# Layer 1's raw weight loads: a pool of four buffers in place of three, and each load issued one part sooner

## The chip, the cores and the metric

The kernel runs on one core of a Trainium2 chip. The metric is the device time of one execution, in microseconds (us); lower is better. Engines are named as in the profile: PE (TensorE), DVE (VectorE), ACT (ScalarE), POOL (GpSimd) and SP, the sequencer on which nearly all DMAs are issued, one after the other.

## What is computed

Two layers over 512 tokens of width 2048, in float32. Layer 0 is forgetting attention, layer 1 is RWKV-7 time mixing; each is a gated branch that is added to x. Layer 1 is the one that the change touches:

```python
def rwkv7_branch(h, v_first, mu, w_in, w0, w1, w2, ...):
    xx = shift(h) - h
    xr, xw, xk, xv, xa, xg = (h + xx * mu[i] for i in range(6))
    r, k, v, z = xr @ w_in[0], xk @ w_in[1], xv @ w_in[2], xg @ w_in[3]
    w = exp(-exp(-softplus(-(w0 + tanh(xw @ w1) @ w2)) - 0.5))
    v = v + (v_first - v) * sigmoid(v0 + (xv @ v1) @ v2)
    a = sigmoid(a0 + (xa @ a1) @ a2)
    kk = l2norm_per_head(k * k_k);  k = k * (1 + (a - 1) * k_a)
    # per head, over time: S = S*w + (S @ -kk) (kk*a)^T + v k^T;  y = S @ r
    ...
    return (group_norm(y) * lnx_w + lnx_b + bonus) * silu(z) @ w_out
```

## The kernel before

Activations lie transposed, a column block of 128 features by 512 tokens. Every big product is made at near float32 precision out of three matmuls in a rounded format: a weight w is split into `whi` (w rounded) and `wlo` (w - whi), an activation into `hi` and `lo`, and `mm3` issues hi*whi, hi*wlo and lo*whi.

**The backbone.** `backbone` walks over a list of weight tiles (2048 x 128). In layer 1 these are 10 tiles of wk1, then 16 each of wr, wv1, wz1 and wo1. A tile comes in four *parts* of 128 x 512 (256 KB), so layer 1 has 296 parts, counted here from 0; one part feeds 12 matmuls. For each part `fetch(n)` does three things in turn: a DMA on SP into a `raw` buffer, then on ACT `whi` = round(raw), then on DVE `wlo` = raw - whi. `raw` has three buffers, `whi` and `wlo` four each. `fetch(n)` is started when the matmuls of part n-4 begin; its ACT step stands 4.5 units of the kernel's own clock later, and not before part n-1 is split and part n-4 used up.

**The order.** The kernel is written out at build time by a small scheduler (`Flow`): tasks yield delays and take turns on a clock that counts PE work alone (`InOrder.clock`). PE, ACT and DVE then execute in the order in which the scheduler wrote them; SP's DMAs stand in one queue as well, in an order that follows it. An instruction that waits holds up all behind it on its engine.

**The side work.** Beside the backbone runs the chain that ends in the recurrence, in `side`: the low-rank products (`lora_k`, `lora_up`; beside wk1), `keys` for 16 blocks (beside wr), `invert` (triangular inverses of four groups, the last of them, group 3, on DVE: tiles `lane` and `lt`) and `inverse`, `stage` (beside wv1), and the chunked recurrence `recur` (beside wv1 and wz1). In `keys` a mean over a head is a pair of PE matmuls `S<-mhi,blkr` and `S<-mlo,blkr`, which wait for `mhi` from ACT and `mlo` from DVE. In `inverse` the matmuls `x<-qt,us` wait for `us` from ACT. In `recur` the tile `xs` is a DVE copy of x that the next PE matmuls (`x<-xs,QP`) read.

Almost all instructions are issued through one helper, so the profile gives them all one line (L90); tiles tell them apart.

Of the kernel before, what the change touches and what calls it, by code (L numbers as in the profile page):

```python
# [9 lines left out]
F = mybir.dt.float32  # L10
R = mybir.dt.float32r
# [6 lines left out]
P = 128  # L18
# [3 lines left out]
WK = 4  # L22
# [109 lines left out]
def body(ctx, tc, a, out, dbg=None, stop=0):  # L132
# [5 lines left out]
    cp = ctx.enter_context(tc.tile_pool(name="cp", bufs=1))  # L138
    wp = ctx.enter_context(tc.tile_pool(name="wp", bufs=4))
    cur = {}  # L140
    ast = ExitStack()
    ctx.callback(ast.close)

# [91 lines left out]
    def split(hi, lo, src):  # L235
        act_hi(hi, src)
        dve.tensor_tensor(out=lo, in0=src, in1=hi, op=OP.subtract)
# [3 lines left out]
        lo = cur["a"].tile([P, T], R, tag="lo", name="lo")  # L241
        return hi, lo

    def wload(src, nk, m, tag="", pool_=None, bufs=None):
        q = pool_ or wp
        raw = q.tile([P, nk, m], F, tag="raw" + tag, name="raw", bufs=bufs or (3 if q is wp else None))
        sp.dma_start(raw, src)
        hi = q.tile([P, nk, m], R, tag="whi" + tag, name="whi", bufs=bufs)
        lo = q.tile([P, nk, m], R, tag="wlo" + tag, name="wlo", bufs=bufs)
        split(hi, lo, raw)  # L250
        return hi, lo

    def mm3(o, w, k, x, first, last, m0=0, m1=P):
        wh, wl = w
        xh, xl = x
        pe.matmul(o, wh[:, k, m0:m1], xh, start=first, stop=False)
        pe.matmul(o, wl[:, k, m0:m1], xh, start=False, stop=False)
        pe.matmul(o, wh[:, k, m0:m1], xl, start=False, stop=last)

    def proj(src, A):  # L260
        o = bank("pj")
        for h in range(0, KT, WK):
            w = wload(src[:, h:h + WK, :], WK, P)
            for k in range(WK):
                mm3(o, w, k, A[h + k], h + k == 0, h + k == KT - 1)
        return o

    mdone = set()

# [49 lines left out]
    def backbone(fl, tiles, at, ready, ends, pairs=(), lead=6, pre=()):  # L319

        units, i = [], 0
        while i < len(tiles):
            us = [[(n, k) for k in range(t[4] if len(t) > 4 else 0, KT)]
                  for n, t in enumerate(tiles[i:i + 1 + (i in pairs)], i)]
            units += us[0][:PLEAD] if len(us) > 1 else us[0]
            for u, v in zip(us[0][PLEAD:], us[1] if len(us) > 1 else ()):
                units += [u, v]  # L330
            if len(us) > 1:
                units += us[1][KT - PLEAD:]
            i += len(us)
        starts = {}
        for i, k in units:
            starts.setdefault((i, k // WK), (i, k))
        parts = list(starts)
        ws, used = {}, set()

        def fetch(n):  # L340
            i, h = parts[n]
            raw = wp.tile([P, WK, P], F, tag="raw", name="raw", bufs=3)
            sp.dma_start(raw, tiles[i][0][:, h * WK:h * WK + WK, :])
            yield 4.5
            while n and parts[n - 1] not in ws or n > 3 and parts[n - 4] not in used:
                yield 0.2
            hi = wp.tile([P, WK, P], R, tag="whi", name="whi")
            lo = wp.tile([P, WK, P], R, tag="wlo", name="wlo")
            act_hi(hi, raw)
            yield 1  # L350
            dve.tensor_tensor(out=lo, in0=raw, in1=hi, op=OP.subtract)
            ws[parts[n]] = hi, lo

        def ending(task, i):
            yield from task
            freed.add(i)

        for n, w in enumerate(pre):
            ws[parts[n]] = w
        for n in range(len(pre), 4):  # L360
            for _ in fetch(n):
                pass
        for n in range(4, len(parts)):
            at.setdefault(starts[parts[n - 4]], []).append(fetch(n))
        last = {id(t[1]): i for i, t in enumerate(tiles)}
        banks, seen = {}, set()
        for i, k in units:
            src, acts, done, j = tiles[i][:4]
            first = i not in seen
            while first and i > 1 and i - 2 not in freed:  # L370
                fl.t += 0.2
                fl.run()
            if first:
                seen.add(i)
                banks[i] = bank("pj")
                at.setdefault((i, max(k, KT - lead)), []).append(ending(done(j, banks[i], i), i))
            for t in at.pop((i, k), ()):
                fl.start(fl.t, t)
            fl.run()
            while (id(acts), k) not in ready or (i, k // WK) not in ws:  # L380
                fl.t += 0.2
                fl.run()
            mm3(banks[i], ws[i, k // WK], k % WK, acts[k], first, k == KT - 1)
            if k % WK == WK - 1:
                used.add((i, k // WK))
            if last[id(acts)] == i:
                spent.add((id(acts), k))
            if k == KT - 1:
                ends.add(i)
# [3 lines left out]
    A = []  # L393
    act_pool("ap0", 16)
    psum("ps0", pj=2, ss=1, S=2, tr=2, pv=1)
    with ExitStack() as s0:
        lq = s0.enter_context(tc.tile_pool(name="lq", bufs=2, reuse_waits="tile"))
        cst, zst = ExitStack(), ExitStack()
# [5 lines left out]
        with tc.tile_pool(name="st0", bufs=2, reuse_waits="tile") as q:  # L404
# [67 lines left out]
            def z_load(n):  # L472
                if n < len(zt):
                    j, g = zt[n]
                    zraw[n] = wp.tile([P, WK, P], F, tag="raw", name="raw", bufs=3)
                    sp.dma_start(zraw[n], a["wz"][j][:, g * WK:g * WK + WK, :])

            def z_split(n):
# [571 lines left out]

    fl = Flow()
    NK = KT - len(ks)
    mq = ctx.enter_context(tc.tile_pool(name="mq", bufs=2, reuse_waits="tile"))
    vst = ExitStack()
    ctx.callback(vst.close)
# [533 lines left out]
    def recur(q):  # L1589
        for m in range(NG * NCH):  # L1590
            g, u, c = m // NCH, m // UC % NU, m % UC
            last = m % NCH == NCH - 1
            while m not in staged or not last and m + 1 not in svs:
                yield 0.1
            if "v" in dbg:
                print("chain", m, fl.t, len(ends))
            yield from hop()
            SV, L, qp, gp, dec, tok = staged.pop(m)
            nSV = None if last else svs[m + 1]
            if c == 0:  # L1600
                y = bank("y")
                y4 = y.rearrange("p (j c t) -> p j c t", j=NJ, c=UC)
            x = bank("x").rearrange("p (a j t) -> p a j t", a=2, j=NJ)
            for j in range(NJ):
                for h in range(2):
                    pe.matmul(x[HS[h], 0, j], L[h][:, j, 0, :], SV[h][:, j, :],
                              start=True, stop=True, skip_group_check=True)
            xs = q.tile([P, NJ, C], F, tag="xs", name="xs", bufs=2)
            dve.tensor_copy(xs, x[:, 0])
            for j in range(NJ):  # L1610
                for h in range(2):
                    pe.matmul(y4[HS[h], j, c], SV[h][:, j, :], L[h][:, j, 1, :],
                              start=j == 0, stop=False, skip_group_check=True)
            for h in range(2):
                s = HS[h]
                for j in range(0 if last else NJ):
                    pool.tensor_scalar(nSV[h][s, j, :], SV[h][s, j, :], dec[s, j, c:c + 1],
                                       1.0, op0=OP.mult, op1=OP.mult)
            yield from hop()
            for j in range(NJ):  # L1620
                for h in range(2):
                    pe.matmul(x[HS[h], 1, j], qp[h][:, j, :], xs[:, j, :],
                              start=True, stop=True, skip_group_check=True)
            for h in range(2):
                dve.tensor_copy(SV[h][HS[h]], x[HS[h], 1])
            yield from hop()
            if not last:
                x = bank("x").rearrange("p (a j t) -> p a j t", a=2, j=NJ)
                for j in range(NJ):
                    for h in range(2):  # L1630
                        pe.matmul(x[HS[h], 0, j], tok[:, j, h, :], SV[h][:, j, :],
                                  start=True, stop=True, skip_group_check=True)
                for h in range(2):
                    s = HS[h]
                    dve.tensor_tensor(out=nSV[h][s], in0=nSV[h][s], in1=x[s, 0], op=OP.add)
            for j in range(NJ):
                for h in range(2):
                    pe.matmul(y4[HS[h], j, c], SV[h][:, j, :], gp[h][:, j, :],
                              start=False, stop=True, skip_group_check=True)
            svs.pop(m)  # L1640
            free["chunk"] += 1
            if c == UC - 1:
                fl.start(fl.t + 0.5, normed(q, g, u, y))
# [216 lines left out]
```

## Time and profile before

| what | value |
|---|---|
| median of 3 runs | 2413.06 us (2410.73 to 2416.13) |
| profiled execution, its own time | 2413.1 us |
| profiled execution, span of the core | 2411.2 us |
| PE busy | 2308.0 us, 96% of the span |
| DVE, ACT, POOL busy | 1605.5, 1257.2, 686.2 us |
| mean bytes moved | 199 GB/s |

PE is the engine that is nearly always busy: what it does not do in the span is 103 us. Busy time of PE is counted from the first to the last of pipelined matmuls, and a matmul at half the clock is busy twice as long, so that the granted clock has to be read beside it.

### The profile page before, as it was taken

To read this page: it belongs to the slowest core of one execution; us is meant where nothing else is said; L and a number is where in the kernel's file an instruction comes from. 1 tells how busy PE (TensorE), PEld (TensorE's weight loads), DVE (VectorE), ACT (ScalarE), POOL (GpSimd) and SP (SyncE) were. 2 spreads that over 40 slices of the span, in tenths; PEclk is the share of its full clock that TensorE was granted. 3 is DMA by queue.
4 is the path that set the end of the run, shared out by engine and by line. 5 is a ranking of instruction groups with operands and counts; after the bars stand their busy time and mean duration, and the time that the engine had idled before them with its cause. 6 is when DMAs were issued, how large, how long until landed. Compare 5 with 4: busy or idle time off the path is not lost. (4 is left out here: it accounts for less than half of the span.)

```text
span 2411.2 us, 39377 instructions
## 1 busy us (share of the span) xinstructions
PE 2308.0 (96%) x13626; PEld 1807.8 (75%) x13626; DVE 1605.5 (67%) x2850; ACT 1257.2 (52%) x2300; POOL 686.2 (28%) x1114
## 2 busy tenths in 40 slices
PE   6999899999999999998999898899999999999999
PEld 4787677877778778886777676677777777777787
DVE  6886678888888745335797567667477776765322
ACT  4435655555565544225646777764345556665221
POOL 0002332533324210110042207771245535450000
PEclk8999999999999999999999999989999999999999
DMA  8864366666666456444755999886867766644543
GB/s 304 329 224 158 108 198 216 212 216 222 201 222 213 133 181 205 137 147 141 227 183 185 301 270 278 262 253 192 237 184 198 212 177 189 173 132 153 160 137 96
DMA packets 388151, 480.22 MB, mean 199 GB/s; under 512 B 146032, under 2 KB 217840, under 8 KB 384112
## 3 DMA queue, kind: packets, MB, share of 16 engines
q1 hardware_dynamic: 386288, 475.08, 63.4%
q0 software_dynamic: 1664, 2.63, 0.3%
q8 instruction: 108, 1.77, 0.3%
q14 instruction: 91, 0.75, 0.1%
HBM read 381.63 MB, written 95.95 MB: 198 GB/s over the span
## 5 line engine op out<-in xcount | busy, mean ns | idle before, releaser
L90 PE MATMUL pj<-hi,whi 128*128 128x512 f32 x2416 | 987.5, 409 | 14.2 <-ACT hi L90 8.2
L90 PE MATMUL pj<-hi,wlo 128*128 128x512 f32 x2416 | 960.2, 397 | 9.1 <-DVE wlo L90 9.1
L90 PE MATMUL pj<-lo,whi 128*128 128x512 f32 x2416 | 960.1, 397 | 0.0
L90 DVE TENSOR_TENSOR wlo<-raw,whi 128x512 fp32r<-128x512 f32 (+2 forms) x628 | 474.5, 763 | 261.4 <-ACT whi L90 258.0
L90 ACT ACTIVATE whi<-raw 128x512 fp32r<-128x512 f32 (+2 forms) x628 | 394.2, 634 | 405.2 <-PE pj L90 229.3
L90 PEld LDWEIGHTS pj<-hi,whi 128*128 128x128 f32 x2416 | 459.6, 190 | 120.4 <-ACT hi L90 9.0
L90 PEld LDWEIGHTS pj<-lo,whi 128*128 128x128 f32 x2416 | 458.4, 190 | 108.7 <-DVE lo L90 0.6
L90 PEld LDWEIGHTS pj<-hi,wlo 128*128 128x128 f32 x2416 | 460.1, 190 | 105.1 <-DVE wlo L90 12.4
L90 DVE CUSTOM_DVE_ANT_0 wm<-wm,cb 128x1024 f32<-128x1024 f32 x128 | 156.7, 1225 | 0.3
L90 POOL TENSOR_SCALAR SV<-SV,dec 64x64 f32<-64x64 f32 x224 | 93.4, 439 | 105.9 <-DVE SV L90 71.7
L90 ACT ACTIVATE pr<-Sm,mx 128x128 f32<-128x128 f32 (+3 forms) x128 | 71.5, 558 | 85.6 <-POOL mx L90 81.6
L90 POOL TENSOR_SCALAR mx<-mx 128x1 f32<-128x1 f32 x128 | 65.7, 513 | 154.9 <-DVE mx L90 118.0
L90 POOL TENSOR_SCALAR pr<-pr,rc 128x128 f32<-128x128 f32 (+3 forms) x128 | 87.6, 685 | 33.0 <-DVE rc L90 28.6
L90 POOL TENSOR_TENSOR lt<-lane 128x30 f32<-128x30 f32 (+14 forms) x90 | 62.7, 697 | 83.9 <-DMA lane<-mld 77.1
L90 DVE CUSTOM_DVE_ANT_0 Sm<-S,cmask 128x128 f32<-128x128 f32 (+3 forms) x128 | 62.0, 484 | 36.0 <-PE S L90 35.4
L90 POOL TENSOR_TENSOR bk<-bk,eI 128x512 f32<-128x512 f32 x32 | 36.1, 1128 | 112.3 <-PE S L90 75.3
L90 POOL TENSOR_TENSOR lane<-lane,lt 128x30 f32<-128x30 f32 (+14 forms) x90 | 65.7, 730 | 7.1
L90 PE MATMUL S<-k,q 128*128 128x128 f32 (+7 forms) x256 | 62.4, 326 | 0.0
L90 PE MATMUL tr<-ident,pr 128*128 128x128 f32 x320 | 57.2, 277 | 4.3 <-DVE pT L90 1.4
L90 POOL TENSOR_TENSOR acc<-acc,sq 128x512 f32<-128x512 f32 x14 | 18.1, 1295 | 150.8 <-ACT sq L90 150.8
L90 PEld LDWEIGHTS tr<-ident,pr 128*128 128x128 f32 x320 | 41.6, 142 | 25.4 <-ACT pT L90 6.9
L90 DVE SCALAR_TENSOR_TENSOR hp<-pj,gate,hp 128x512 f32<-128x512 f32 x16 | 12.0, 751 | 68.9 <-PE pj L90 68.9
(325 smaller groups left out, 3272.8 us busy)
## 6 DMA issues: line engine op xcount, KB each, us to landing
wm<-in_wmodT SPq DMA_DIRECT2D x132, 512.0 KB, 4.3
raw<-in_wz SPq DMA_DIRECT2D x128, 256.0 KB, 3.8
raw<-in_wo SPq DMA_DIRECT2D x128, 256.0 KB, 3.5
raw<-in_wv SPq DMA_DIRECT2D x124, 256.0 KB, 3.8
wm<-in_wmodT SPq DMA_DIRECT2D x30, 1024.0 KB, 6.9
raw<-in_wk SPq DMA_DIRECT2D x96, 256.0 KB, 3.7
raw<-in_wr SPq DMA_DIRECT2D x64, 256.0 KB, 5.1
raw<-in_wq SPq DMA_DIRECT2D x56, 256.0 KB, 3.6
```

Source lines behind the costliest of these rows:

```text
L90: self.last = f(*a, **k)
```

## The change

`raw` leaves the pool `wp` and gets a pool of its own, made anew for each layer: three buffers in layer 0, four in layer 1. `fetch(n)` is started at part n-1-`cur["rn"]`: part n-4 as before in layer 0, part n-5 in layer 1. To make room (a raw buffer takes 2 KB of each partition), `xs` of the recurrence has one buffer in place of two. Two helpers that nothing called (`wload`, `proj`) are gone.

```diff
+    def raw_pool(name, bufs):
+
+        rst.close()
+        cur["r"] = rst.enter_context(tc.tile_pool(name=name, bufs=bufs, reuse_waits="tile"))
+        cur["rn"] = bufs
...
         def fetch(n):
             i, h = parts[n]
-            raw = wp.tile([P, WK, P], F, tag="raw", name="raw", bufs=3)
+            raw = cur["r"].tile([P, WK, P], F, tag="raw", name="raw")
             sp.dma_start(raw, tiles[i][0][:, h * WK:h * WK + WK, :])
...
         for n in range(4, len(parts)):
-            at.setdefault(starts[parts[n - 4]], []).append(fetch(n))
+            at.setdefault(starts[parts[max(0, n - 1 - cur["rn"])]], []).append(fetch(n))
...
+    raw_pool("rw0", 3)
...
-                    zraw[n] = wp.tile([P, WK, P], F, tag="raw", name="raw", bufs=3)
+                    zraw[n] = cur["r"].tile([P, WK, P], F, tag="raw", name="raw")
...
     NK = KT - len(ks)
+    raw_pool("rw1", 4)
...
-            xs = q.tile([P, NJ, C], F, tag="xs", name="xs", bufs=2)
+            xs = q.tile([P, NJ, C], F, tag="xs", name="xs", bufs=1)
```

PE's order is the same in both kernels. What moves are the DMAs on SP and the splits on ACT and DVE. Three places follow.

SP, where the parts of wk1 end and those of wr begin (`ip`, `kt`, `aa` are the loads of the first block of `keys`). Before:

```order
694 L90 DMA hp<-mxd 128x512 x3
695 L90 DMA raw<-in_wk 128x512
696 L90 DMA ip<-ipd 128x4x128
697 L90 DMA kt<-kTd 128x512
698 L90 DMA aa<-aad 128x512
699 L90 DMA raw<-in_wr 128x512
700 L90 DMA hp<-mxd 128x512 x3
701 L90 DMA raw<-in_wr 128x512
```

With the change:

```order
692 L90 DMA hp<-mxd 128x512 x3
693 L90 DMA raw<-in_wr 128x512
694 L90 DMA ip<-ipd 128x4x128
695 L90 DMA kt<-kTd 128x512
696 L90 DMA aa<-aad 128x512
697 L90 DMA raw<-in_wr 128x512
698 L90 DMA hp<-mxd 128x512 x3
699 L90 DMA raw<-in_wr 128x512
```

The rows of loads stand in the same places, but each carries the next part: where the last part of wk1 stood there is now the first of wr. So it is in the whole of layer 1: nearly every other DMA has one raw load more ahead of it.

ACT, at the sixth block of `keys` (`sq`, `eI`, `aa`, `mhi`, `t` are its steps; `r<-pj` and `m<-hp` belong to other tasks). Before:

```order
1149 L90 ACTIVATE whi<-raw 128x512
1150 L90 ACTIVATE gab<-S 64x256 x4
1151 L90 ACTIVATE sq<-kt,vecs 128x512
1152 L90 ACTIVATE eI<-ip 128x8x64
1153 L90 ACTIVATE whi<-raw 128x512
1154 L90 ACTIVATE aa<-aa,oka,vecs 128x512
1155 L90 ACTIVATE r<-pj 128x512
1156 L90 ACTIVATE mhi<-sq 128x512
1157 L90 ACTIVATE m<-hp,omu 128x512
1158 L90 ACTIVATE whi<-raw 128x512
```

With the change:

```order
1146 L90 ACTIVATE whi<-raw 128x512
1147 L90 ACTIVATE gab<-S 64x256 x4
1148 L90 ACTIVATE whi<-raw 128x512
1149 L90 ACTIVATE sq<-kt,vecs 128x512
1150 L90 ACTIVATE eI<-ip 128x8x64
1151 L90 ACTIVATE aa<-aa,oka,vecs 128x512
1152 L90 ACTIVATE whi<-raw 128x512
1153 L90 ACTIVATE r<-pj 128x512
1154 L90 ACTIVATE mhi<-sq 128x512
```

The split that stood behind `eI` now stands ahead of `sq`, and the one that stood behind `m` now stands ahead of `r` and `mhi`. In 9 of the 16 blocks of `keys` one split more stands ahead of `mhi`.

DVE, where the inversion of group 3 begins (`lt`, `lane`; `lo<-hp` is a split of an activation). Before:

```order
1782 L90 STREAM_TRANSPOSE t_15902<-qt_13171 32x256
1783 L90 TENSOR_TENSOR wlo<-raw,whi 128x512
1784 L90 TENSOR_TENSOR lt<-lane 128x30
1785 L90 TENSOR_TENSOR lane<-lane,lt 128x30
1786 L90 TENSOR_TENSOR lo<-hp,hi 128x512
1787 L90 TENSOR_TENSOR wlo<-raw,whi 128x512
1788 L90 TENSOR_TENSOR lt<-lane 128x58
```

With the change:

```order
1788 L90 STREAM_TRANSPOSE t_15912<-qt_13181 32x256 x2
1789 L90 TENSOR_TENSOR wlo<-raw,whi 128x512 x2
1790 L90 TENSOR_TENSOR lt<-lane 128x30
1791 L90 TENSOR_TENSOR lane<-lane,lt 128x30
1792 L90 TENSOR_TENSOR lo<-hp,hi 128x512
1793 L90 TENSOR_TENSOR wlo<-raw,whi 128x512
1794 L90 TENSOR_TENSOR lt<-lane 128x58
```

Part 99's `wlo` stood behind the first `lt` (row 1787 before); now it stands ahead of it, together with part 98's, and the row behind carries part 100.

## Rows read from the trace of the kernel before

**Rows 1.** The page's head: span and busy time of each engine.

```profile
span 2411.2 us, 39377 instructions
PE 2308.0 (96%) x13626; PEld 1807.8 (75%) x13626; DVE 1605.5 (67%) x2850; ACT 1257.2 (52%) x2300; POOL 686.2 (28%) x1114
```

**Rows 2.** Stretches: length, busy (count) by engine, granted clock, DMA share, GB/s.

```profile
1140.00:1200.00 60.00, 60.00 (x260) 48.66 (x259) 44.60 (x61) 42.54 (x66) 3.66 (x10) 1.00 0.79 239
...
1366.00:1600.00 234.00, 210.87 (x1360) 162.31 (x1360) 161.16 (x206) 169.74 (x312) 134.87 (x185) 0.96 0.90 264
1600.00:1660.00 60.00, 53.19 (x451) 41.18 (x450) 43.37 (x91) 27.45 (x55) 24.07 (x33) 0.91 0.73 222
1660.00:1760.00 100.00, 95.28 (x855) 75.80 (x855) 48.32 (x91) 37.29 (x73) 16.92 (x40) 0.98 0.83 221
1760.00:2160.00 400.00, 387.69 (x3882) 303.75 (x3878) 287.83 (x615) 236.55 (x410) 198.78 (x378) 0.99 0.66 182
...
2280.00:2340.00 60.00, 60.00 (x259) 48.27 (x258) 16.71 (x25) 13.29 (x21) 0.00 (x0) 1.00 0.46 137
```

**Rows 3.** Waits of PE, 1366 to 1600: us in total, times, longest.

```profile
PE S L90 <- DVE mlo L90: 11.0, 11, 1.9
PE S L90 <- ACT mhi L90: 9.3, 6, 3.7
PE x L90 <- ACT us L90: 2.9, 4, 1.0
```

**Rows 4.** Waits of ACT, then of SP's queue, 1366 to 1600.

```profile
ACT whi L90 <- DMA raw<-in_wr: 30.9, 20, 3.4
...
SPq L90 <- DVE kk L90: 13.3, 15, 2.1
SPq L90 <- DVE wlo L90: 5.7, 11, 1.4
```

**Rows 5.** Timeline of SP, ACT and PE, 1444 to 1461: start, duration, instruction [wait].

```profile
1444.83 0.52 SPq L90 DMA_DIRECT2D rTd<-r  x1
...
1448.05 0.86 SPq L90 DMA_DIRECT2D raw<-in_wr  x1
...
1459.88 1.06 SPq L90 DMA_DIRECT2D raw<-in_wr  x1
...
1453.68 0.63 ACT L90 ACTIVATE whi<-raw 128x512 fp32r<-128x512 f32 x1 [3.41 <-DMA raw<-in_wr]
...
1456.72 0.50 PE L90 MATMUL S<-mhi,blkr 128*128 128x512 f32 x1 [1.05 <-ACT mhi L90]
1458.35 0.50 PE L90 MATMUL S<-mlo,blkr 128*128 128x512 f32 x1 [1.12 <-DVE mlo L90]
```

**Rows 6.** Timeline of PE at another block of keys, 1482 to 1486.

```profile
1484.11 0.50 PE L90 MATMUL S<-mlo,blkr 128*128 128x512 f32 x1 [1.11 <-DVE mlo L90]
```

**Rows 7.** Timeline of DVE and PE, 1603 to 1623, and PE's waits, 1600 to 1660.

```profile
1616.55 0.19 DVE L90 TENSOR_TENSOR lt<-lane 128x30 f32<-128x30 f32 x1 [10.02 <-DMA lane<-mld]
...
1619.30 0.50 PE L90 MATMUL pj<-hi,wlo 128*128 128x512 f32 x1 [1.38 <-DVE wlo L90]
...
1621.94 0.80 PE L90 MATMUL pj<-hi,wlo 128*128 128x512 f32 x1 [1.67 <-DVE wlo L90]
...
PE pj L90 <- DVE wlo L90: 6.1, 4, 1.7
```

**Rows 8.** Waits of PE, 1660 to 1760, and timeline of ACT there.

```profile
PE S L90 <- ACT mhi L90: 3.9, 1, 3.9
...
1745.29 0.63 ACT L90 ACTIVATE whi<-raw 128x512 fp32r<-128x512 f32 x1 [3.50 <-DMA raw<-in_wv]
```

**Rows 9.** Waits of PE and of ACT, 1760 to 2160.

```profile
PE S L90 <- ACT GP L90: 8.3, 5, 4.1
...
ACT whi L90 <- PE pj L90: 34.3, 21, 3.7
```

**Rows 10.** Timeline of ACT at the start of layer 1's backbone.

```profile
1189.62 0.63 ACT L90 ACTIVATE whi<-raw 128x512 fp32r<-128x512 f32 x1 [4.20 <-DMA raw<-in_wk]
```

More of the change, by code (lines that the diff above doesn't have):

```diff
@@ L140, in body @@
     cur = {}
+    rst = ExitStack()
+    ctx.callback(rst.close)
+    def raw_pool(name, bufs):
+        rst.close()
+        cur["r"] = rst.enter_context(tc.tile_pool(name=name, bufs=bufs, reuse_waits="tile"))
+        cur["rn"] = bufs
     ast = ExitStack()
@@ L242, in new_act @@
         return hi, lo
[L244 to L251, printed above, removed]
     def mm3(o, w, k, x, first, last, m0=0, m1=P):
@@ L258, in mm3 @@
         pe.matmul(o, wh[:, k, m0:m1], xl, start=False, stop=last)
[L260 to L266, printed above, removed]
     mdone = set()
```

## The prediction

> **What bounds the kernel now.** I read the page's head first: PE is busy for 2308.0 of 2411.2 us [rows 1], so the whole kernel can gain at most the 103 us in which PE idles, plus what PE loses to a lower clock. Then I cut the span into stretches. Layer 0 keeps its three buffers and its order, so only the time from about 1180 us on can move. There PE is full at both ends: 60.00 of 60.00 us just ahead of layer 1's backbone, and 60.00 of 60.00 in the output product [rows 2]. The idle time lies between: 23.1 us in 1366 to 1600 (`keys` beside wr), 6.8 in 1600 to 1660 (the inversion of group 3), 4.7 in 1660 to 1760 (the first `stage`), 12.3 in 1760 to 2160 (the recurrence) [rows 2]. In the same stretches the granted clock is below 1: 0.96, 0.91, 0.98 and 0.99, which is 9.4, 5.4, 2.0 and 4.0 us of full-speed work that PE did not do [rows 2].
>
> Next, who ends PE's waits. In 1366 to 1600 it is never the backbone's own weights: PE waits 20.3 us for `mlo` and `mhi` of the means in `keys`, and 2.9 us for `us` [rows 3]. ACT, which makes `mhi` and `us`, is not full (169.74 of 234 us [rows 2]); it stands 30.9 us, in 20 waits, at a `whi` whose raw part has not landed [rows 4]. One such place shows the chain: SP issues a raw load at 1448.05; ACT reaches its split and waits 3.41 us, until 1453.68; `mhi` comes late behind it, PE waits 1.05 us for `mhi` and 1.12 us for `mlo` [rows 5]. So a late load costs PE time because ACT works in order, although the part itself is not needed yet. The load is late because its turn on SP comes late: SP waits for a free raw buffer (`wlo`) for 5.7 us only, against 13.3 us for the buffers of `kt` [rows 4]. What helps here is the earlier place in the queue; the fourth buffer is what allows it.
>
> **The change, part by part.** *The load.* One part sooner in layer 1 is about three other DMAs sooner. From 1444.83 to 1460.94 the timeline has 16 rows on SP, 4 of them raw loads (the first and the last row stand in [rows 5]): one per 4.0 us, and that is what one place further up the list of loads is worth at most. *The split.* It moves too. It stood 4.5 units behind the start of part n-4; now the load is issued a part earlier, its 4.5 units are over sooner, and what holds the split is only that part n-4 be used up. In 9 of 16 blocks of `keys` one 0.63 us split [rows 5] more stands ahead of `mhi`. The net slack of a load is thus the move on SP less the move of the split. The trace of before has neither; between 0 and 4.0 us I take half, 2.0, which is above the mean ACT wait of 30.9/20 = 1.5 us [rows 4], so that most of these waits should end.
>
> *Term A, 1366 to 1600.* PE has 11 waits for `mlo` [rows 3], one in each of 11 blocks of `keys`. One of these blocks has no wait of ACT for a load ahead of it, and PE still waits 1.11 us for `mlo` [rows 6]. I let every block keep that: 20.3 - 11 x 1.11 = 8.1 us go, and the 2.9 us for `us`, which stands in the same queue on ACT, go as well: -11.0 us (bounds 0 and -23.2, all of [rows 3]). Which waits cost PE its clock the rows don't tell; I let half of the 9.4 us come back: -4.7 (bounds 0 and -9.4). Against that, 9 splits ahead of `mhi` at 0.63 us are 5.7 us, of which half falls into time in which PE has other work: +2.8 (bounds 0 and +5.7).
>
> *Term B, 1600 to 1660.* PE waits 6.1 us in four waits for `wlo` [rows 7]. DVE stood 10.02 us at the first `lt` for its DMA and part 99's `wlo` was queued behind it; PE's first two waits, 1.38 and 1.67 us, follow [rows 7]. With the change part 99 stands ahead of that `lt`, and part 100 at part 99's old place, so these two go: -3.05. The second pair falls into a time in which DVE is full of `lt` and `lane`; I leave it. Half of the 5.4 us of clock: -2.7. Sum -5.8 (bounds 0 and -11.5).
>
> *Term C, 1660 to 1760.* PE's one long wait is 3.9 us for a `mhi`, and ACT had stood 3.50 us at a `whi` [rows 8]. Half of 3.9 and half of the 2.0 us of clock: -3.0 (bounds 0 and -5.9).
>
> *Term D, 1760 to 2160.* Here ACT waits for PE rather than for loads: 34.3 us in 21 waits at `whi`, 1.6 each, and PE's waits behind ACT's `GP` are 8.3 us [rows 9]. An earlier split waits longer with others behind it. The trace does not show by how much; I take +2.0, about a quarter of the 8.3 (bounds 0 and +20, worked out under the rivals).
>
> *Edits that cost nothing.* The start: ACT waits 4.20 us for part 3's load [rows 10]; that load now stands among the first four, ahead of the stage before, and the wait ends, but PE was full until then [rows 2], so nothing is gained. `xs` with one buffer: its next copy waits for the matmuls that read the last one, and these stand ahead of the matmuls that make the next x on PE anyway; without that cover it would be a wait of under 1 us for each of 32 chunks. The output product: PE is full [rows 2] and stays so. The unused helpers issue nothing.
>
> Sum: -11.0 - 4.7 + 2.8 - 5.8 - 3.0 + 2.0 = -19.7 us. The profiled execution took 2413.1 us, 1.9 outside its span of 2411.2, and the median is 2413.06, so no correction: 2393.4, say **2394 us**. Its own range: with half of A and B unrealised 2403; with the second pair and all of the clock 2383.
>
> **Room on the DMA side.** The DMA engines are busy for 0.90 of 1366 to 1600 [rows 2], 211 us of work. If it is the same work, the stretch can't become shorter than that: A is at most -23.4. At -12.9 net the share would be 0.95. That is close enough to full for the extra landing time to eat some of it.
>
> **The rivals.** *Half of it.* The loads come sooner, the splits take most of it back in `keys` (A nets about 0), B and some of C stay: 2413.1 - 5.8 - 2 = 2405 us. For it: splits and loads move by the same rule. Against it: split and load need not move alike, since the split is held by its part's use.
>
> *Nothing.* SP is the limit. The 16 rows from 1444.83 to 1460.94 [rows 5] add up to 13.4 us of issue in 16.1 us; if it is the row itself that is full, a load taken forward puts everything else back by one load, `kt` and `aa` come late in their turn, and `mhi` waits for these: 2413 us, within 5. Against it: among ACT's waits in this stretch is none for `kt` or `aa`, so these have slack to give. The Trainium skill (Perfetto Trace Analysis, What "DMA-bound" means) calls a kernel DMA-bound when the issuing sequencer's track is solid with DMA slices, and names larger descriptors as what matters then; by it, an earlier place would give nothing, 2413, and not 2394. The 13.4 of 16.1 us come near to it.
>
> *Slower.* In the recurrence ACT reaches `whi` ahead of PE, as it already does 21 times. Each earlier split makes `GP`, `mhi`, `L` or (on DVE) `xs` behind it late by a split of 0.63 us [rows 5], in the recurrence and in `keys` alike, so that A nets 0 as well. If every one of 32 chunks pays it on PE's path it is 32 x 0.63 = 20 us; with B and C halved (-4.4) that is 2429. It decides from 7 chunks on (7 x 0.63 = 4.4), as long as A does not come. Taken at half the chunks: +10 - 4.4, 2419 us. For it: PE waits for `GP` at five places already [rows 9]. Against it: PE idles only 12.3 of 400 us there [rows 2], so most delays have cover now.
>
> **How the numbers follow.** The likeliest, 2394 (2383 to 2403): 0.44. Half of it, 2405 (2402 to 2408): 0.18. Nothing, 2413 (2408 to 2418): 0.20. Slower, 2419 or more: 0.15. Still faster than 2383: 0.03. About 0.2% (4.8 us) is what a measurement of this kernel can tell from no change. Faster by more than that: 0.44 + 0.18 + 0.03 = 0.65; within: 0.20; slower: 0.15. The range 2384 to 2415 leaves out the slow case and the far end of the fast one, under 2 in 10.
>
> **What would show it.** ACT's waits for raw parts in wr fall from 30.9 us to under 10, PE's idle time in `keys` from 23 to about 12 us with a clock nearer 1, and the two waits at the first `lt` are gone: then the steps hold. If ACT's waits for loads go and PE's waits for `mlo` stay, A was wrong in what a block keeps. If the loads land no sooner, SP or the DMA engines are full. If waits of PE for `GP`, `xs` or `mhi` behind 1760 us grow by more than 5 us, the slow rival is there.

## The result, and the profile after

The changed kernel took 2415.78 us in the median of 20 runs, the kernel before 2410.66 in 20 runs on the same chip: a ratio of 1.0021 (95%: 1.0014 to 1.0029). It is 0.2% slower. The prediction said 2394 us, and gave "slower" a chance of 0.15. Two executions below, of 4473.16 us (the kernel before) and 5680.99 us (raw_five), fell into a slower state and are left out of every median and ratio.

The page of the changed kernel has the same work in the same span, within a few us of [rows 1]:

```profile
span 2412.5 us, 39387 instructions
PE 2307.3 (96%) x13626; PEld 1810.2 (75%) x13626; DVE 1599.5 (66%) x2850; ACT 1259.1 (52%) x2300; POOL 692.5 (29%) x1114
```

The stretches of [rows 2] after the change (length, busy time and count of PE, PEld, DVE, ACT and POOL, granted clock, DMA share, GB/s):

```profile
1366.00:1600.00 234.00, 211.94 (x1366) 163.43 (x1365) 160.16 (x207) 173.37 (x316) 136.87 (x184) 0.96 0.92 265
1600.00:1660.00 60.00, 51.21 (x448) 39.47 (x447) 43.48 (x91) 26.73 (x54) 24.53 (x33) 0.94 0.74 220
1660.00:1760.00 100.00, 98.19 (x882) 78.47 (x881) 49.44 (x95) 39.06 (x77) 19.09 (x43) 0.98 0.82 225
1760.00:2160.00 400.00, 386.68 (x3858) 302.62 (x3858) 283.44 (x608) 237.00 (x408) 199.58 (x377) 0.99 0.65 182
```

PE's idle time in `keys` is 22.1 us where 12 were forecast, and it was 23.1 before. So the page already says that term A did not come. The waits say more. Of ACT in 1366 to 1600, against [rows 4]:

```profile
ACT whi L90 <- DMA raw<-in_wr: 15.8, 12, 2.2
ACT m L90 <- DMA hp<-h1d: 10.0, 9, 2.9
```

The raw parts do land sooner for ACT: 30.9 us of waiting became 15.8 (under 10 were forecast). But 7.7 us of it stand now at another load, `hp` of `h1d`, which was 2.3 us in two waits before. And PE's waits there, against [rows 3], then behind 1760, against [rows 9], and ACT's in the recurrence:

```profile
PE S L90 <- DVE mlo L90: 11.1, 12, 3.5
PE S L90 <- ACT mhi L90: 6.9, 4, 3.5
...
PE S L90 <- ACT GP L90: 10.3, 6, 7.5
...
ACT whi L90 <- PE pj L90: 69.2, 50, 3.7
```

`mlo` has not moved (11.0 before). In the recurrence ACT stands twice as long as before at a `whi` whose buffer PE has not given back: 69.2 us in 50 waits against 34.3 in 21. PE's own waits behind 1760 have hardly grown (`GP` by 2.0 us). Two places that the forecast named came as it said, and they hardly show in the time: DVE's first `lt` waits 5.43 us where it was 10.02 in [rows 7], with part 99's `wlo` now ahead of it, and ACT no longer waits for part 3 at the start [rows 10] (the last row here is parts 0 to 3, split one after the other):

```profile
1610.95 0.69 DVE L90 TENSOR_TENSOR wlo<-raw,whi 128x512 fp32r<-128x512 f32 x1 [3.82 <-ACT whi L90]
1617.08 0.19 DVE L90 TENSOR_TENSOR lt<-lane 128x30 f32<-128x30 f32 x1 [5.43 <-DMA lane<-mld]
...
1183.06 2.18 ACT L90 ACTIVATE whi<-raw 128x512 fp32r<-128x512 f32 x4
```

To compare kernels whose times shift against each other I cut the backbone by its own parts. It is PE's last 3552 matmuls into `pj`, 12 for each of 296 parts (four k tiles by three products), so the first matmul of a part can be counted off in any trace (where two tiles take turns, the count stands for the matmul at that place). Parts 28 to 84 are `lora` and `keys` (1308 to 1559 us in the kernel before), 84 to 132 the inversions and the first stage, 132 to 216 the recurrence (1738 to 2173).

| kernel | 28 to 84 | 84 to 132 | 132 to 216 | 216 to 292 |
|---|---|---|---|---|
| before | 251.8 | 178.4 | 435.2 | 223.1 |
| changed | 254.6 | 180.1 | 432.8 | 224.7 |
| changed, second trace | 253.1 | 181.4 | 432.6 | 225.1 |

These two traces of one program differ by up to 1.5 us in such a piece, but one trace can be further off: before_late and before_mix below, whose ACT, DVE and SP run the same order up to 1540 us, took 221.2 and 227.5 us for parts 28 to 80. So a gain or a loss of 2 us in a piece, as in the recurrence and in `keys` here, can be the noise of one execution; what several kernels show alike counts. The question is why half of ACT's waits for raw parts could go without any gain.

### The profile page after: what moved, and what is told of

Same layout as the page of the kernel before. It is cut to its first block, busy times and chain, and to the rows that moved or that the text cites. A ratio compares the mean times of both kernels' runs of the same rounds, so it can differ in the third digit from the quotient of the medians.

```text
span 2412.5 us, 39387 instructions
## 1 busy us (share of the span) xinstructions
PE 2307.3 (96%) x13626; PEld 1810.2 (75%) x13626; DVE 1599.5 (66%) x2850; ACT 1259.1 (52%) x2300; POOL 692.5 (29%) x1114
## 5 line engine op out<-in xcount | busy, mean ns | idle before, releaser
L90 POOL TENSOR_SCALAR mx<-mx 128x1 f32<-128x1 f32 x128 | 65.6, 513 | 153.9 <-DVE mx L90 116.6
L90 ACT ACTIVATE hi<-hp 128x512 fp32r<-128x512 f32 x62 | 38.4, 626 | 35.4 <-PE pj L90 16.5
```

The lines of the kernel that those rows point to most:

```text
L90: self.last = f(*a, **k)
```

## The experiments

Three theories. **Theory 1**, the rival "Nothing": SP's row is full, and every other load of layer 1, which now has one raw load more ahead of it, comes late in its turn; the waits for `h1d` speak for it. **Theory 2**, the rival "Slower": the splits (`whi` on ACT, `wlo` on DVE) moved ahead with their loads, and the work of `keys` and of the recurrence stands behind them. **Theory 3**: the buffers themselves, the new pool's addresses or `xs` with one buffer.

### The change in pieces: four_only, load_only, split_only, after_again

`four_only` takes the changed kernel and puts load and split back:

```diff
-            at.setdefault(starts[parts[max(0, n - 1 - cur["rn"])]], []).append(fetch(n))
+            at.setdefault(starts[parts[n - 4]], []).append(fetch(n))
```

> The pool of four raw buffers and xs with one buffer as in the change, but load and split of each part stay where they stood before. Theory 1 (the place of the load in SP's row costs: every other load of layer 1 has one raw load more ahead of it, and what then comes late holds up ACT and PE as the raw load did) and theory 2 (the earlier place of the splits on ACT and DVE costs): within 0.1% of before, since neither place is changed. Theory 3 (the buffers themselves: other addresses, xs with one buffer): slower than before by 0.2%, about 5 us, as the changed kernel is. ACT's waits for raw parts stay near 31 us in 20 in 1366 to 1600.

`load_only` takes the changed kernel and parts the load from the split. Only the load stays a part sooner:

```diff
         def fetch(n):
             ...
             sp.dma_start(raw, tiles[i][0][:, h * WK:h * WK + WK, :])
+            raws[n] = raw
+
+        def cutting(n):
+            raw = raws.pop(n)
             yield 4.5
             ...
-            at.setdefault(starts[parts[max(0, n - 1 - cur["rn"])]], []).append(fetch(n))
+            at.setdefault(starts[parts[max(0, n - 1 - cur["rn"])]], []).append(loading(n))
+            at.setdefault(starts[parts[n - 4]], []).append(cutting(n))
```

> The changed kernel with its loads one part sooner, but with each split back at its place before. Theory 1: no faster than the changed kernel, 2413 to 2418 us; ACT's waits for raw parts near 10 us or less in wr, and its waits for h1d and mxd loads stay at about 10 and 11 us, as in the changed kernel. Theory 2: the raw waits go without the price of the earlier splits, so faster than before by 5 to 15 us, 2395 to 2406 us.

`split_only` takes the kernel before, its loads and three buffers, and asks for the split at once:

```diff
-            yield 4.5
+            yield 0.1 if len(tiles) == 74 else 4.5
```

> The kernel before with three buffers and its loads in place, and in layer 1 each split asked for as soon as its load is issued and its place is free, as the changed kernel does. Theory 1: the other loads keep their places, so the waits for h1d and mxd stay near 2.5 us each; ACT reaches the splits sooner and waits longer for raw parts, 31 us in wr growing to 40 or more; 0 to 10 us slower than before for that reason alone. Theory 2: slower by 5 us or more with ACT's raw waits unchanged, through later GP, mhi and L.

`after_again` is the changed kernel for a second trace.

> The changed kernel once more, for a second trace of it: what returns in it is the kernel's, what differs is one execution's. Theory 1: waits of ACT for h1d and mxd loads again at about 10 us each in layer 1 against 2.5 before, raw waits in wr again near 16 us, 1.002 of before.

The four groups of experiments ran on four chips, each beside the kernel before; where kernels of two groups are compared, each is taken against the kernel before on its own chip. (A ratio is taken over the executions, not from the two medians, and can differ from theirs by up to 0.1%.) Measured here (before: 2412.51 us): four_only 2412.76, ratio 0.9997 (0.9987 to 1.0008). load_only 2399.78, **0.9948** (0.9935 to 0.9961). split_only 2453.1, **1.017** (1.0148 to 1.0191). after_again 2414.29, 1.001 (1.0 to 1.0019).

Theory 3 falls with four_only. Theory 1 falls with load_only: the loads are as early as in the changed kernel and nearly every other load is as late, and it gains 12.7 us. By the traces, 853 of 935 other DMAs from layer 1 on stand behind the same raw load in both kernels, and all of those that are issued in 1366 to 1600 do; ACT and DVE run the order of the kernel before. ACT's waits for loads, 1366 to 1600, in load_only:

```profile
ACT m L90 <- DMA hp<-h1d: 23.4, 13, 3.6
...
ACT hi L90 <- DMA hp<-mxd: 6.0, 3, 4.0
...
ACT whi L90 <- DMA raw<-in_wr: 1.4, 2, 0.8
```

The wait for `h1d` that looked like the culprit in the changed kernel is 23.4 us here, in the faster kernel. I read it as the place where ACT now arrives early. All of ACT's waits for loads in this stretch add up to 34.8 us before, 27.1 in the changed kernel and 30.8 in load_only: the faster of the last two waits longer, so their sum is no price. What differs between the two kernels is, but for those few DMAs, the split's place, and that is worth 14.5 us (2414.29 against 2399.78). PE's waits for `mlo`, the largest in [rows 3], are nearly halved by it:

```profile
PE S L90 <- ACT mhi L90: 8.4, 4, 3.1
PE S L90 <- DVE mlo L90: 5.8, 7, 2.0
```

split_only shows the other side. With the loads where they were, the earlier split waits longer for them, and PE waits longer for `mhi` and `mlo` (ACT's waits, then PE's, 1366 to 1600):

```profile
ACT whi L90 <- DMA raw<-in_wr: 49.0, 25, 4.7
...
PE S L90 <- ACT mhi L90: 15.9, 9, 3.7
PE S L90 <- DVE mlo L90: 15.2, 12, 2.9
```

Parts 28 to 84 took 272.9 us there. My expectation for theory 2, that ACT's raw waits would stay, was wrong in form: they grew as theory 1 had it, and the time with them, by 40.6 us where theory 1 had 0 to 10. Load and split do not add: the earlier load is worth 12.7 us with the split at its old place and 38.8 with the split early (2453.1 against 2414.29).

### Later still, and which half: late_split, before_late, hi_early, early_keys

`late_split` is load_only, and `before_late` the kernel before with its three buffers, each with this edit:

```diff
-            yield 4.5
+            yield 6.5 if len(tiles) == 74 else 4.5
```

> Loads one part sooner, as in the change, and each split of layer 1 two units of the backbone's clock later than in the kernel before (6.5 in place of 4.5). If what counts is that work of the recurrence and of keys stands ahead of the splits on ACT and DVE (theory 2), and the splits still have slack to their part: faster than load_only by 2 to 6 us, 2394 to 2398. If the splits have no more slack: PE waits for whi and wlo, which were near 0, and it is slower than load_only by 5 us or more.

> The kernel before, three buffers, loads in place, with each split of layer 1 at 6.5 in place of 4.5. If the gain of load_only is nothing but the time between a load and its split, this has it too: 2398 to 2404 us, and ACT's raw waits in wr fall from 38.7 to under 15. If the place of the load counts for itself, or a later split gives the buffer back too late for the load after next, 2408 to 2415, as before.

`hi_early` is load_only with `whi` made where the changed kernel makes it, and `wlo` later, at its old place:

```diff
+        def early(n):
+            yield from rounding(n, fetch(n))
             ...
-            at.setdefault(starts[parts[max(0, n - 1 - cur["rn"])]], []).append(loading(n))
-            at.setdefault(starts[parts[n - 4]], []).append(cutting(n))
+            at.setdefault(starts[parts[max(0, n - 1 - cur["rn"])]], []).append(early(n))
+            at.setdefault(starts[parts[n - 4]], []).append(rest(n))
```

> Loads one part sooner; the half of each split on ACT (whi) at its place in the changed kernel, the half on DVE (wlo) at its place in the kernel before. If the earlier place costs on ACT: 2411 to 2416, as the changed kernel. If it costs on DVE: 2399 to 2403, as load_only. In between where both do.

`early_keys` is load_only with part of the splits at the early place:

```diff
-            at.setdefault(starts[parts[n - 4]], []).append(cutting(n))
+            e = len(tiles) == 74 and 28 <= n < 84
+            at.setdefault(starts[parts[n - 4 - e]], []).append(cutting(n))
```

> load_only with the splits of parts 28 to 83 (keys, from about 1305 to 1570 us) back at their earlier place, as in the changed kernel; the rest late. Theory 2 by the traces: load_only and the changed kernel differ by 4.6 us in parts 40 to 84 and 2.7 in 28 to 40, the remainder behind; so 2405 to 2408 us. If the price lies in the recurrence (parts 104 on): within 3 us of load_only.

Measured (before: 2410.64): late_split 2402.77, 0.9965 (0.9952 to 0.9978). before_late 2399.78, **0.9957** (0.9942 to 0.9972). hi_early 2414.03, **1.0017** (1.0005 to 1.003). early_keys 2405.09, 0.9975 (0.9966 to 0.9984).

The one line of before_late gains 10.9 us without a fourth buffer and with no load taken forward; its interval overlaps that of load_only. ACT's raw waits in `keys` fall to 4.5 us by it:

```profile
ACT m L90 <- DMA hp<-h1d: 17.7, 10, 3.4
...
ACT hi L90 <- DMA hp<-mxd: 7.2, 5, 3.7
...
ACT whi L90 <- DMA raw<-in_wr: 4.5, 7, 1.7
```

So it helps when ACT does not come to a split before its part has landed, and no difference was measured between a sooner load and a later split. before_late does not part this from the split's place, for in 9 of 16 blocks of `keys` it also has one split less ahead of `mhi` than the kernel before; load_only has the old places. hi_early has the price whole with DVE's half at its old place (none of the 16 blocks has more `wlo` ahead of `mlo` than before): the price is paid on ACT. early_keys puts 7.2 us of it into parts 28 to 84 by the medians, 7.9 by the trace (255.2 against 247.3). late_split is my second case, or just short of it (5 us), 4.9 us behind load_only by the medians, and its trace shows where: parts 84 to 104, in which DVE makes `lt` and `lane`, took 85.1 us against 78.8.

### What ACT stands for: whi_five and at_one, and a mixture

In the recurrence the changed kernel's ACT stands at `whi` for PE's buffer. `whi_five` is the changed kernel with a fifth buffer for `whi` in layer 1; the room comes from `at` and `sq`, which have one buffer instead of two. `at_one` has these two edits alone.

```diff
-            hi = wp.tile([P, WK, P], R, tag="whi", name="whi")
+            hi = (cur["x"] if len(tiles) == 74 and n % 5 == 4 else wp).tile([P, WK, P], R, tag="whi", name="whi")
```

> The changed kernel, order of all engines as it is, with a fifth buffer for whi in layer 1, so that a split on ACT no longer stands until PE has used the part four ahead (the room comes from at and sq with one buffer each). In the changed kernel ACT stands 30 us in 17 waits in parts 84 to 132 and 78 us in 59 waits in parts 132 to 216 at whi for PE; in load_only 22 and 43 us. If these waits are the price of the earlier split: they go, and the time falls to that of load_only where they stood, 2403 to 2408 us. If the price is the place in the row alone (0.63 us of a split, or its wait for a load, ahead of mhi and GP): within 2 us of at_one.

> The changed kernel with at and sq of one buffer each and four whi buffers, the control for whi_five: 2413 to 2417 us, as the changed kernel, if those two buffers cost nothing.

`load_mix` is load_only, and `before_mix` the kernel before, with the split late where it was better late:

```diff
-            yield 4.5
+            yield 6.5 if len(tiles) == 74 and (n < 84 or 104 <= n < 216) else 4.5
```

> load_only with the splits of parts below 84 and of parts 104 to 215 at 6.5 and the others at 4.5, each where the traces had it shorter: parts 84 to 104 took 78.8 us with 4.5 and 85.1 with 6.5, the rest of it differs by under 2 us in all. Summed by parts from the traces of load_only and late_split 2393 to 2396 us; if the parts don't add, 2400 as load_only.

> The same two places of the split with the loads and the three buffers of the kernel before. Summed by parts from the traces of before and before_late: 2392 to 2395 us (parts 216 to 240 fall from 80.1 to 77.5, parts 84 to 104 from 81.8 to 78.4). If the place of the load has a worth of its own, 3 us or more above load_mix; if only the time between load and split counts, within 3 us of it.

Measured (before: 2410.93): whi_five 2408.29, 0.9991 (0.998 to 1.0002). at_one 2415.7, 1.0012 (1.0003 to 1.0022). load_mix **2396.48**, 0.994 (0.9926 to 0.9954). before_mix 2398.97, 0.9951 (0.9938 to 0.9964).

The fifth buffer gives 7.4 us against its control. ACT's waits at `whi` in 1760 to 2160, in at_one and then in whi_five:

```profile
ACT whi L90 <- PE pj L90: 67.1, 50, 3.7
```

```profile
ACT whi L90 <- PE pj L90: 5.8, 3, 3.1
```

In parts 132 to 216 whi_five took 427.5 us and at_one 433.6; in parts 28 to 84 it gained nothing (256.9 against 255.8). That is about half the price of the early split, and it shows the mechanism: ACT comes to a split whose `whi` buffer PE still reads, and all that stands behind it on ACT waits with it. load_mix, 0.6% faster than the kernel before, is the best version that ran; it is not told from load_only (0.994 and 0.9948, intervals that overlap), and it came 0.5 us above my sum. before_mix came 4 us above its sum, so there the parts did not add.

### What is left in keys: raw_five and early_rec

`raw_five` keeps the order of ACT and DVE of the changed kernel (by the traces it is the same) and lets the loads go a part sooner again (five raw buffers, `at` and `sq` with one), so that no split should wait for its part:

```diff
-            at.setdefault(starts[parts[n - 4]], []).append(cutting(n))
+            e = cur["rn"] == 5
+            at.setdefault(starts[parts[max(0, n - 4 - e)]], []).append(cutting(n))
...
-    raw_pool("rw1", 4)
+    raw_pool("rw1", 5)
```

> The order of ACT and DVE as in the changed kernel, the loads of layer 1 one part sooner again, with five raw buffers (the room from at and sq with one buffer, as in at_one). ACT's waits for raw parts in wr and wv fall from 15 us each to under 3. If these waits were what is left of the price in keys: faster than at_one by 4 to 6 us, 2409 to 2412, in parts 28 to 84. If it is the place of the split ahead of mhi, or the wait for a whi buffer: within 2 us of at_one, 2414 to 2418, and parts 40 to 84 stay at 173 to 175 us.

`early_rec` is early_keys for parts 132 to 215 in place of 28 to 83.

> load_only with the splits of parts 132 to 215 (the recurrence, from about 1740 to 2150 us) back at their earlier place, the rest late. By the traces the changed kernel took 4.4 us more there than load_only, by whi_five against at_one the waits for a whi buffer cost 6 us: 2404 to 2407 us, and ACT's waits at whi for PE there back from 43 to 75 us. If within 2 us of load_only, the loss in the recurrence is not its own but follows from what was late ahead of it.

Measured (before: 2410.86): raw_five 2417.77, **1.0027** (1.0015 to 1.0039). early_rec 2402.77, 0.9968 (0.9956 to 0.998). Against the kernel before on its chip early_rec is 4.6 us behind load_only, and ACT's waits at `whi` for PE in 1760 to 2160 went from 38.7 to 72.6 us, about as expected; the time, 2402.77 us, is 1.2 us under the range that I had.

raw_five has no wait for a raw part of wr left, and it is no faster than at_one. Its longest waits of ACT for loads in 1366 to 1600, and PE's:

```profile
ACT m L90 <- DMA hp<-h1d: 14.3, 8, 2.8
...
ACT hi L90 <- DMA hp<-mxd: 5.8, 3, 4.8
...
PE S L90 <- DVE mlo L90: 8.9, 11, 2.7
PE S L90 <- ACT mhi L90: 8.4, 5, 3.7
```

So the waits for raw parts that the changed kernel still has are not what is left of the price. What is left is the place of the split in ACT's row. That is by exclusion: ACT still stands 20.1 us here for `h1d` and `mxd`, but it stands longer for them (29.4) in the faster load_only. All pieces together, by falling ratio:

| kernel | loads ahead by | split | ratio | 28 to 84 | 132 to 216 |
|---|---|---|---|---|---|
| split_only | 4 parts | early | 1.017 | 272.9 | 438.4 |
| raw_five | 6 parts | early | 1.0027 | 258.8 | 435.3 |
| changed | 5 parts | early | 1.0021 | 254.6 | 432.8 |
| hi_early | 5 parts | early on ACT | 1.0017 | 252.2 | 436.8 |
| at_one | 5 parts | early | 1.0012 | 255.8 | 433.6 |
| four_only | 4 parts | at 4.5 | 0.9997 | 252.1 | 433.6 |
| whi_five | 5 parts | early, 5 `whi` | 0.9991 | 256.9 | 427.5 |
| early_keys | 5 parts | early in 28 to 83 | 0.9975 | 255.2 | 427.3 |
| early_rec | 5 parts | early in 132 to 215 | 0.9968 | 244.5 | 432.3 |
| late_split | 5 parts | at 6.5 | 0.9965 | 246.1 | 426.1 |
| before_late | 4 parts | at 6.5 | 0.9957 | 244.7 | 425.3 |
| before_mix | 4 parts | 6.5 or 4.5 | 0.9951 | 249.6 | 429.7 |
| load_only | 5 parts | at 4.5 | 0.9948 | 247.3 | 428.4 |
| load_mix | 5 parts | 6.5 or 4.5 | 0.994 | 246.3 | 426.7 |

Wherever the split is early, `keys` takes 252 us or more, as it does where the load is late for the split (four_only); where the split is late enough for its load, 244 to 250. The recurrence divides in the same way (432 us and more against 425 to 430), but for whi_five, where the buffer is free. The gap between the groups is smaller than what one trace can be off, so this rests on the groups and not on a row.

## Why the prediction was wrong

**The step that failed** is "The split. It moves too", with the prices that came from it. I gave the moved split 2.8 us in term A and 2.0 us in term D, 4.8 in all, and let the loads gain 24.5. By load_only the earlier loads are worth 12.7 us (2412.51 to 2399.78), and by load_only against after_again the moved split costs 14.5. The loads gained half of what I had, the splits cost three times as much, and 1.8 us to the bad was left on that chip (5.1 in the result above). The slack itself was sized well: I took 2.0 us between load and split, and in the traces the mean time from a load's issue to its `whi` in parts 28 to 84 grew from 7.2 to 10.0 us. What I had wrong is what the split does from its new place.

**The second step that failed** is the clock. Of the 24.5 us, 8.4 were half of the lost clock (4.7, 2.7 and 1.0 in A, B and C), and they did not come. Worked out as in the prediction, the four stretches lost 20.8 us to the clock before, 19.0 and 21.4 in the two traces of the changed kernel, and 21.8 in load_only, where waits of PE did go. "Which waits cost PE its clock the rows don't tell" was right, and half was a term without a reason.

**Term A** (-12.9 net). The chain that I read from [rows 5] is real: a late load holds ACT, and `mhi` and `mlo` come late behind it. load_only took PE's waits for `mlo` from 11.0 to 5.8 us in 1366 to 1600, all of [rows 3] from 23.2 to 15.0, and parts 28 to 84 from 251.8 to 247.3. But the change moves the split as well: by the trace one split more stands ahead of `mhi` in 10 blocks of `keys`. raw_five shows that with this order PE's waits for `mlo` stay at 8.9 us with not one raw wait left. [Rows 6], the block that waited without a raw wait ahead of it, was the hint. I took it as a floor of 1.11 us for each block, and load_only, with 5.8 us in 7 waits, shows that it was none.

**Term B** (-5.8). PE's waits for `wlo` fell from 6.1 us in four to 3.5 in two, about the total that was forecast, but in part by luck. The first pair is gone, but a new wait of 1.92 us stands at 1627.89; of the second pair, which I had left, one wait of 1.63 us is there, at 1640.68. The second trace has 4.7 us in four waits, one of them 1.51 us at 1619.34. Beside them PE stands 3.8 us for `t` in the inversion (its waits, 1600 to 1660; 1.3 us in the second trace):

```profile
PE x L90 <- DVE t L90: 3.8, 3, 2.4
PE pj L90 <- DVE wlo L90: 3.5, 2, 1.9
```

Parts 84 to 104 took 75.9 us where they took 78.4 (77.6 in the second trace), and 104 to 132 gave it back, 104.3 against 100.0.

**Term C** (-3.0). PE's one long wait for `mhi`, 3.9 us in [rows 8], is 1.5 us now, as half had it; the clock stood at 0.98 as before. The stretch gained 2.9 us of busy PE, but parts 104 to 132 as a whole took longer.

**Term D** (+2.0). The place and the direction were right, the size was not: 34.3 us of ACT's waits for PE became 69.2, and the price of the early split there is 4.6 us by early_rec and about 6 by whi_five. It did not show as the forecast asked (waits of PE for `GP`, `xs` or `mhi` growing by more than 5 us behind 1760): the recurrence became 2.4 us shorter than before by the trace, where load_only makes it 6.8 shorter. A price that eats a gain leaves no row of its own here; the kernel without it shows it.

**The start**, which I put at nothing, gave some 2 us by the traces: parts 0 to 28 took 116.6 us before and 114.5 and 114.6 in the two traces of the changed kernel.

**The rivals.** "Slower" named this mechanism. It priced a split at its 0.63 us for each chunk, while in the recurrence, by the traces, the price went whole with a fifth `whi` buffer (427.5 us in whi_five, 428.4 in load_only). "Nothing" rested on SP's full row, and the measured 2415.78 us lies in its band (2408 to 2418); that is luck, for two effects of over 12 us each nearly cancel. Other loads did come late (the wait for `h1d` went from 2.3 to 10.0 us), but this is not what costs the time. By the Trainium skill (Perfetto Trace Analysis, What "DMA-bound" means) one of the things that a DMA-bound kernel can be bound on is the issuing sequencer, whose track is then solid with DMA slices. The 13.4 of 16.1 us here were short of that. before_late issues the same loads in much the same row and gains 0.43%, so the row was not the bound here. raw_five, with still earlier loads, is 2.1 us worse than at_one, each against the kernel before on its chip (the ratios' intervals overlap). That would fit a price of that row; no run here tells it apart.

**What stays open.** Of the 14.5 us, early_keys accounts for 7.2 and early_rec for 4.6 by the medians (7.9 and 3.9 by the traces); the remainder lies in parts that no run moved alone, or within what the medians can tell. How one split ahead of `mhi` turns into the wait for `mlo` on DVE within a block of `keys` was not followed further; that the split's work ahead of `mhi` is what costs in `keys` is argued by exclusion.

## What to carry to other kernels

A load's lead over its use has two ends: the instruction that issues it, and the first instruction that needs it on an engine that works in order. Before a buffer is bought for an earlier load, try that instruction later: one line gained 10.9 us here, and the fourth buffer with the split left in place 12.7. And if load and first use hang on one task, moving the task moves both, and the use then waits for the other thing that it needs (here the buffer that PE still reads), with the whole engine behind it.

A wait that grows after a change is not yet its price. `h1d` on ACT grew to 10.0 us in the slower kernel and to 23.4 in the faster one.

## What the runs showed of the hardware

Nothing new of the chip itself was needed to explain the time. The granted clock did not tell the three main kernels apart: it was 0.96 in 1366 to 1600 in the kernel before, in the changed one and in load_only alike, though PE's busy time there was 210.87, 211.94 and 216.56 us. Only split_only was lower, 0.93 at 200.92 us.
